# Six of the eight gate units of a retention mixer as three pairs by seven products, with the token sums kept in the retention results' memory

## The chip, the cores and the metric

The kernel runs on one core of a Trainium2 chip. It is one step of a small hybrid decoder: 512 prompt tokens and 8 sample tokens go through two layers. The metric is the device time of one execution in microseconds (us).

## The reference, cut to what matters

The change lies in the first layer's mixer, where the gate `g` is one of six parts of a combined input projection:

```python
h = rmsnorm(x, norm_mix_g[l])
z = h @ w_in                                   # (520 tokens, 1024) @ (1024, 5120)
q, k, v, g, u, s = jnp.split(z, SPLIT_IDX, axis=-1)   # widths 512, 512, 1024, 1024, 1024, 1024
...
o_n = ((o - mu) * lax.rsqrt(var + LN_EPS)).reshape(b, t, V_W) * gn_g
ret_out = jax.nn.silu(g) * o_n
```

All numbers are float32. The norm's factor is a number per token, so the kernel multiplies the weights by unnormalised rows and applies the factor `r0` to the products.

## The kernel before

**Layout.** Channels lie on the 128 partitions, tokens along the row: `x0` is [128, 8 chunks of channels, 520 tokens]. The 520 tokens are split into two halves of 260 columns (`HALF`), since a TensorE product writes one bank.

**A unit** is 128 output channels. Its weights arrive as one 512 KB transfer into `raw` (four buffers). `split` makes them into a high and a low part for half of the input channels at a time: ScalarE rounds (`wh`, L134), VectorE subtracts (`wl`, L135), each 128x512. The inputs are split in the same way into `n0h` and `n0l`. TensorE multiplies high by high, high by low and low by high: 8 chunks x 3 products x 2 halves = 48 matmuls of 260 columns, all in `unit_mm` (L163).

**A pair by seven products** is what the feed-forward stage uses already (`Pair`, `run`, L251). Two units whose weights form a 2x2 block matrix, by output unit and half of the input channels, meet tokens that form another, by half of the channels and half of the tokens. Seven products of sums in place of eight: 7 x 4 chunks x 3 = 84 matmuls instead of 96. It needs four sums of weights (`S`, VectorE, L236 to L239, 128x512 each), seven splits instead of four, the sums of tokens (`Tokens`, `T` high and low), and sums of the results, which are read from the banks `pp`, `pq`, `pr`. Products 2, 3 and 1 go on unsummed tokens; 5, 7, 6 and 4 on `Th`, `Tl`. Product 4 is left pending and done in the next pair, or by `flush`.

**Token sums** (`Tokens.sums(k)`, four calls): ScalarE scales one row (`Tu`, L206), VectorE makes four sums of 260 (`t4`, L209 to L212), and for two halves of the result ScalarE rounds (`Th`, L216) and VectorE subtracts (`Tl`, L217), 128x520 each.

**The stage around the change.** After the norm, units follow in this order: four for `k`, four for `q`, eight for the gate `g`, eight for `v`. For each `q` unit ScalarE makes two copies of 64 rows (`sw`), GpSimd multiplies `sw` by sines (L478) and later the result by `xi` (L489), and VectorE does the rest (L477, L479, `qm` L494, `qk_s` L618). For each gate unit VectorE multiplies the bank by `r0` (L502), ScalarE takes Silu (L503, with a load of its table before the first), and GpSimd multiplies by the norm's gain (L504) into `sg`.

**Order.** A scheduler at build time sets each engine's order and the semaphores; each engine then runs its list strictly in that order. **Memory.** The tag `big` has five buffers: `x0`, `n0h`, `n0l`, `sg`, `reth`, and `retl` takes the place of `x0`, whose last reader was the norm.

Of the kernel before, what the change touches and what calls it, by code (L numbers as in the profile page):

```python
# [6 lines left out]
F32 = mybir.dt.float32  # L7
F32R = mybir.dt.float32r
I32 = mybir.dt.int32
AF = mybir.ActivationFunctionType  # L10
ALU = mybir.AluOpType
# [3 lines left out]
P = 128  # L15
D = 1024
C = 8
TP = 512
TS = 8
T = TP + TS  # L20
HALF = T // 2
# [57 lines left out]
def trunk_kernel(tc, a, o):  # L79
    nc = tc.nc  # L80
    te, ve, se, pe_ = nc.tensor, nc.vector, nc.scalar, nc.gpsimd
    with ExitStack() as st:
# [10 lines left out]
        def open_stage(name):  # L93
            stage.close()
            return stage.enter_context(tc.tile_pool(name=name, bufs=2, reuse_waits="tile"))

        mp = open_stage("mix0")

        def bigt(name, dt=F32):
            return big.tile([P, C, T], dt, name=name, tag="big")  # L100
# [4 lines left out]
        def mmt(name):  # L105
            return ps.tile([P, 2, 512], F32, name=name, tag="mm", bufs=2)
# [10 lines left out]
        def h2(ap):  # L117
            return ap.rearrange("p (h t) -> p h t", h=2)

        def ph2(pt):  # L120
            return pt[:, :, :HALF]
# [7 lines left out]
        KH = C // 2  # L129
# [14 lines left out]
        def halves(pt):  # L144
            return [pt[:, hf, :HALF] for hf in range(2)]
# [9 lines left out]
        def unit_mm(pts, w, x, mid=None, ks=range(C), all_ks=None):  # L155

            order = list(all_ks or ks)
            for n, k in enumerate(ks):
                hi, lo = w[k // KH]
                for i in range(3):  # L160
                    wt = lo if i == 2 else hi
                    for hf in range(2):
                        last = te.matmul(pts[hf], wt[:, k % KH, :], x(k, SECOND if hf else FIRST)[i == 1],  # L163
                                         start=k == order[0] and i == 0, stop=k == order[-1] and i == 2)
                if mid and n == 4:
                    mid()
            return last

        def unit(pt, ap, row, col, x, mid=None, ks=range(C)):

            return unit_mm(halves(pt), split_w(load_w(ap, row, col)), x, mid=mid, ks=ks)
# [15 lines left out]

        T_OF = {5: 0, 7: 1, 6: 2, 4: 3}

        def four(name):  # L190
            return mp.tile([P, 4, HALF], F32, name=name, tag="f4", bufs=2)

        class Tokens:


            def __init__(self, x, nm):
                self.x, self.nm = x, nm
                self.b = two(nm.hi, nm.lo)
                self.t = [mp.tile([P, C, T], F32R, name="T" + s, tag="T", bufs=2)
                          .rearrange("p (k a) (b t) -> p k (a b) t", k=KH, b=2) for s in "hl"]  # L200

            def sums(self, k):
                t4 = four("t4")
                x, g1, g2 = self.x, pcol(self.nm.g, k), pcol(self.nm.g, KH + k)
                u = tmp("Tu")
                se.activation(u, x[:, k, :], AF.Copy, scale=g1)  # L206
                b21, b22 = x[:, KH + k, FIRST], x[:, KH + k, SECOND]
                stt = ve.scalar_tensor_tensor
                ve.tensor_sub(t4[:, 0], u[:, FIRST], u[:, SECOND])  # L209
                stt(out=t4[:, 1], in0=b22, scalar=g2, in1=u[:, SECOND], op0=ALU.mult, op1=ALU.subtract)  # L210
                stt(out=t4[:, 2], in0=b22, scalar=g2, in1=t4[:, 0], op0=ALU.mult, op1=ALU.add)
                stt(out=t4[:, 3], in0=b21, scalar=g2, in1=t4[:, 2], op0=ALU.mult, op1=ALU.subtract)  # L212
                hi, lo = [t[:, k] for t in self.t]
                for i, sign in enumerate((1.0, -1.0)):
                    s = slice(2 * i, 2 * i + 2)
                    se.activation(hi[:, s], t4[:, s], AF.Copy, scale=sign)  # L216
                    stt(out=lo[:, s], in0=t4[:, s], scalar=sign, in1=hi[:, s].bitcast(F32), op0=ALU.mult, op1=ALU.subtract)  # L217
# [39 lines left out]
        def flush():  # L257
            while pending:
                pending.pop().product(4)

        def run(pair, mid=None):
            if not pair.w:
                pair.load()
            pair.open()
            pair.product(1)
            flush()
            for n in (2, 3, 5, 6, 7) if pair.early else (2, 5, 6, 3, 7):
                if mid and n == (5 if pair.early else 3):
                    mid()
                pair.product(n)  # L270
            pending.append(pair)
# [11 lines left out]
        x0 = bigt("x0")  # L283
# [3 lines left out]
        def pcol(i, c):  # L287
            return par[:, i, c:c + 1]
# [121 lines left out]
        W_IN = a["ab_w_in"]  # L410
# [7 lines left out]
        nm = Norm(G_MIX0, "n0")  # L418
# [5 lines left out]
        xs0 = two(nm.hi, nm.lo)  # L424
# [12 lines left out]
        r0 = nm.r  # L437
# [13 lines left out]
        def in_units(first, n):  # L451
            for j in range(n):
                if first == 512 and j < 3:
                    pt = (k0, pt1, pt2)[j]
                else:
                    pt = mmt(f"in{first}_{j}")
                    unit(pt, W_IN, 0, first + j * P, xs0)
                yield j, pt
# [4 lines left out]
        def rot(pt, name, flat=False):  # L463
            sw = tmp(name + "sw")
            y = mp.tile([P, 544], F32, name=name, tag="qk", bufs=8)[:, :T]
            if isinstance(pt, list):
                parts = [(pt[hf], slice(hf * HALF, (hf + 1) * HALF)) for hf in range(2)]
            elif flat:
                parts = [(pt, slice(0, T))]
            else:  # L470
                parts = [(ph2(pt), None)]
            for src, cols in parts:
                def v(ap):
                    return h2(ap) if cols is None else ap[:, cols]
                se.copy(v(sw)[0:64], src[64:128])
                se.copy(v(sw)[64:128], src[0:64])
                ve.tensor_tensor(v(y), src, v(cs[:, 0, :]), op=ALU.mult)  # L477
            pe_.tensor_mul(sw, sw, cs[:, 1, :])  # L478
            ve.tensor_add(y, y, sw)  # L479
            return y  # L480

        kt, qt = [], []
        for h, pt in in_units(512, NH):
            y = rot(pt, f"k{h}", flat=h == 0)
            ve.tensor_scalar(ks[:, h, :], y[:, TP:], KSCALE, None, op0=ALU.mult)
            kt.append(y)
        for h, pt in in_units(0, NH):
            y = rot(pt, f"q{h}")
            pe_.tensor_tensor(y[:, :TP].rearrange("p (n t) -> p n t", n=NC), y[:, :TP].rearrange("p (n t) -> p n t", n=NC),  # L489
                              xi[:, h:h + 1, :].to_broadcast([P, NC, P]), op=ALU.mult)  # L490
            qt.append(y)
# [4 lines left out]


        sg = bigt("sg")
        reth, retl = bigt("reth", F32R), bigt("retl", F32R)
        for c, pt in in_units(2048, C):  # L500
            t = tmp(f"g{c}")
            ve.tensor_tensor(h2(t), ph2(pt), h2(r0), op=ALU.mult)  # L502
            se.activation(sg[:, c, :], t, AF.Silu)  # L503
            pe_.tensor_scalar(sg[:, c, :], sg[:, c, :], pcol(GN_G, c), None, op0=ALU.mult)  # L504


        def tok(n):
# [78 lines left out]
        for c, pt in in_units(1024, C):  # L586
            vT = tmp(f"vT{c}")
            ve.tensor_tensor(h2(vT), ph2(pt), h2(r0), op=ALU.mult)
            pe_.tensor_copy(vs_sm[:, c, :], vT[:, TP:])
            if prev:  # L590
                v_tok(*prev)
            prev = c, vT
            h = c // 2
            if c % 2 == 0:
                if h:
                    on[h - 1] = ret_head(h - 1, *pk[h - 1])
                if h > 1:
                    ret_gate(h - 2, on[h - 2])
                pk[h] = ret_scores(h)
# [99 lines left out]
        for hf in range(2):  # L699
            for i in range(2):  # L700
                t = mp.tile([P, 544], F32, name="ln_row", tag="qk", bufs=8)[:TS, :512]
# [37 lines left out]
        for c, pt in in_units(4096, C):  # L739
            t = tmp(f"s{c}")  # L740
# [18 lines left out]
        x = bigt("x")  # L759
# [13 lines left out]
        for c in range(2, C):  # L773
            pt = mmt(f"opr{c}")
# [14 lines left out]
        for c, pt in in_units(3072, C):  # L789
            g = c // 2  # L790
            t = tmp(f"u{c}")
            bias_c = mp.tile([P, TP], F32, name="bias_c", tag="on", bufs=4)[:, :P]
            ve.scalar_tensor_tensor(out=bias_c, in0=ws[:, g, :], scalar=pcol(SLN_B, c), in1=bias_row[:, g, :],
                                    op0=ALU.mult, op1=ALU.add)
# [3 lines left out]
            for n in range(NC):  # L798
# [6 lines left out]
                                    op0=ALU.mult, op1=ALU.add)  # L805
# [9 lines left out]
        for i in range(2):  # L815
            ht = mp.tile([P, nk, C, TS], F32, name="hist", tag="vtm", bufs=NH)
            nc.sync.dma_start(ht, a["hist"][:, i * nk:(i + 1) * nk])
            for c in range(C):
                pe_.tensor_tensor(ht[:, :, c, :], ht[:, :, c, :],
                                  dw[:, c, i * nk:(i + 1) * nk].rearrange("p (k o) -> p k o", o=1).to_broadcast([P, nk, TS]),  # L820
                                  op=ALU.mult)
# [6 lines left out]
        mp = open_stage("ffn0")  # L828


        nm = Norm(G_FFN0, "n1", eng=ve)
        x7 = Tokens(x, nm)
        ahead = Pair(a["ffn_w1"][0], 0, [u * KH * P for u in range(2)], x7, None, True)
        for c in BY_PAIR:
            if c == 2:
                ahead.load()
            pt = mmt(f"ops{c}")
# [135 lines left out]
        mp = open_stage("mix1")  # L973
# [4 lines left out]
        for c in range(CFULL, C):  # L978
            tag, bufs, parts = (("kx", 2, 2), ("s0", 3, 1), ("s0", 3, 1), ("s0", 3, 1), ("S", 1, 1))[c - CFULL]
            for i in range(parts):  # L980
                n = NS // parts
# [159 lines left out]
        mp = open_stage("ffn1")  # L1141
# [37 lines left out]
        nm = Norm(G_FFN1, "n3", eng=ve)  # L1179
        x7 = Tokens(x, nm)  # L1180
# [72 lines left out]
```

## Time and profile before

| | |
|---|---|
| runs, us | 1302.75, 1303.93, 1305.08 (median 1303.93) |
| the profiled execution | 1304.76 us, its span 1303.0 us |
| busy, share of the span | TensorE 98%, VectorE 68%, ScalarE 49%, GpSimd 14% |
| TensorE's mean granted clock | 0.993 |

The profile is of one execution. A row of a timeline gives start, duration, engine, line, operation, tiles and shapes, and in brackets how long the engine had been idle and for whom. A duration contains a part that overlaps the next instruction of the same engine, so what an engine can do in a stretch is read from the distance of two starts. In rows of groups, the number after the bar is busy time, then the mean duration in ns.

### The profile page before, as it was taken

What the parts mean: (1) busy time and instruction counts of PE and PEld (TensorE: products, weight loads), DVE (VectorE), ACT (ScalarE), POOL (GpSimd) and SP (SyncE); (2) the same over time, 40 slices, a digit from 0 to 9 for tenths busy, and PEclk for the clock granted to TensorE, in tenths of its full rate; (3) what the DMA queues carried; (4) which work ended last, traced back from release to release, by engine and by line L of the source; (5) the groups of instructions that cost most, each with busy time, mean ns of one, the idle gap of its engine ahead of it and who ended that gap; (6) DMA issues with size and microseconds to landing.
All of it is one profiled execution on the core that took longest, in us unless ns stands there. A gap on an engine that the chain in (4) does not pass through costs nothing.

```text
span 1303.0 us, 26234 instructions
## 1 busy us (share of the span) xinstructions
PE 1271.8 (98%) x10736; PEld 1237.5 (95%) x10736; DVE 891.2 (68%) x1628; ACT 638.7 (49%) x1148; POOL 183.1 (14%) x188
## 2 busy tenths in 40 slices
PE   9999999999999999999999999999899999999996
PEld 8999998999999999999999999868799999999996
DVE  6833667747888866766655799737987667576544
ACT  7433343335466644544434466347765445454342
POOL 0521012213000000000000479412000000000010
PEclk9999999999999999999999999999899999999998
DMA  8233235576423333333333324545333323332321
GB/s 284 88 92 97 76 111 182 177 233 224 137 81 99 98 98 98 98 100 96 98 98 98 93 87 118 147 99 149 110 98 98 114 82 108 104 98 81 98 81 66
DMA packets 51176, 149.62 MB, mean 115 GB/s; under 512 B 6081, under 2 KB 14401, under 8 KB 51057
## 3 DMA queue, kind: packets, MB, share of 16 engines
q1 hardware_dynamic: 46528, 134.37, 33.9%
q0 software_dynamic: 3456, 12.58, 2.9%
q8 instruction: 84, 1.38, 0.4%
q10 hardware_dynamic: 1072, 1.00, 0.2%
q14 instruction: 36, 0.29, 0.1%
HBM read 139.47 MB, written 9.41 MB: 114 GB/s over the span
## 4 chain that ended last, share of the span: by engine, by line
PE 86%; DVE 6%; POOL 4%; issue 2%; ACT 2%; DMA 0%; SPq 0%; DVEq 0%; ACTq 0%; POOLq 0%
PE y L163 27%; PE in L163 16%; PE pp L251 13%; PE pq L251 6%; POOL pacc L1052 3%; PE pr L251 3%; PE ops L163 3%; PE opr L163 3%; PE ci L163 2%; PE co L181 2%; PE f L163 2%; DVE wl L135 1%; PE cvB L1029 1%; PE cvA L1029 1%; PE opr L181 1%
## 5 line engine op out<-in xcount | busy, mean ns | idle before, releaser
L134 ACT ACTIVATE wh<-raw 128x512 fp32r<-128x512 f32 x378 | 237.0, 630 | 341.2 <-PE in L163 102.9
L135 DVE TENSOR_TENSOR wl<-raw,wh 128x512 fp32r<-128x512 f32 x378 | 274.5, 729 | 162.7 <-ACT wh L134 159.7
L163 PE MATMUL y<-f,wh 128*128 128x260 f32 x2016 | 324.0, 283 | 0.8 <-DVE x L912 0.8
L163 PEld LDWEIGHTS y<-f,wh 128*128 128x128 f32 x2016 | 275.7, 188 | 1.2 <-DVE x L912 1.2
L163 PE MATMUL y<-f,wl 128*128 128x260 f32 x1008 | 202.6, 282 | 0.0
L163 PEld LDWEIGHTS y<-f,wl 128*128 128x128 f32 x1008 | 155.3, 188 | 0.0
L163 PE MATMUL in<-n0h,wh 128*128 128x260 f32 x640 | 133.3, 288 | 1.4 <-DVE k L477 0.8
L163 PE MATMUL in<-n0l,wh 128*128 128x260 f32 x640 | 130.8, 285 | 1.0 <-DVE n0l L366 0.9
L163 PE MATMUL in<-n0h,wl 128*128 128x260 f32 x640 | 129.6, 284 | 0.1
L134 ACT ACTIVATE wh<-S 128x512 fp32r<-128x512 f32 x120 | 75.7, 632 | 96.6 <-PE y L163 45.6
L135 DVE TENSOR_TENSOR wl<-S,wh 128x512 fp32r<-128x512 f32 x120 | 82.2, 688 | 50.7 <-ACT wh L134 49.6
L163 PEld LDWEIGHTS in<-n0h,wh 128*128 128x128 f32 x640 | 99.0, 189 | 4.0 <-issue 1.9
L251 PE MATMUL pp<-Th,wh 128*128 128x260 f32 x360 | 101.9, 283 | 0.0
L251 PE MATMUL pp<-Tl,wh 128*128 128x260 f32 x360 | 101.4, 282 | 0.0
L251 PE MATMUL pp<-Th,wl 128*128 128x260 f32 x360 | 101.1, 282 | 0.0
L163 PEld LDWEIGHTS in<-n0l,wh 128*128 128x128 f32 x640 | 98.8, 188 | 2.4 <-DVE n0l L366 2.1
L163 PEld LDWEIGHTS in<-n0h,wl 128*128 128x128 f32 x640 | 98.5, 188 | 0.4 <-DVE wl L135 0.3
L251 PEld LDWEIGHTS pp<-Th,wh 128*128 128x128 f32 x360 | 67.9, 189 | 0.3 <-ACT wh L134 0.2
L251 PEld LDWEIGHTS pp<-Tl,wh 128*128 128x128 f32 x360 | 67.8, 188 | 0.1
L251 PEld LDWEIGHTS pp<-Th,wl 128*128 128x128 f32 x360 | 67.4, 188 | 0.0
L865 ACT ACTIVATE f<-f 128x520 fp32r<-128x520 f32 x60 | 38.4, 640 | 50.2 <-DVE f L864 50.2
L1052 POOL TENSOR_TENSOR pacc<-pacc,pp 128x512 f32<-128x512 f32 x39 | 59.5, 1530 | 4.0 <-ACT pp L1051 1.7
(410 smaller groups left out, 2771.9 us busy)
## 6 DMA issues: line engine op xcount, KB each, us to landing
raw<-in_ffn_w SPq DMA_DIRECT2D x128, 512.0 KB, 3.7
raw<-in_ab_w_in SPq DMA_DIRECT2D x39, 512.0 KB, 3.7
S<-in_state_ret POOLq DMA_DIRECT2D x16, 512.0 KB, 4.6
raw<-in_ab_w_out SPq DMA_DIRECT2D x16, 512.0 KB, 3.7
raw<-in_conv_w_in SPq DMA_DIRECT2D x16, 512.0 KB, 3.7
raw<-in_conv_w_out SPq DMA_DIRECT2D x16, 512.0 KB, 3.9
X<-xscr SPq DMA_DIRECT2D x40, 132.0 KB, 3.5
x<-in_xT SPq DMA_DIRECT2D x16, 260.0 KB, 4.5
```

The lines of the kernel that those rows point to most:

```text
L134: se.activation(hi, sp, AF.Copy)
L135: ve.tensor_sub(lo, sp, hi.bitcast(F32))
L163: last = te.matmul(pts[hf], wt[:, k % KH, :], x(k, SECOND if hf else FIRST)[i == 1], start=k == order[0] and i == 0, stop=k == order[-1] a ...
L181: te.matmul(pt, wt[:, k % KH, :], xt, start=n == 0 and i == 0, stop=n == C - 1 and i == 2)
L251: te.matmul(bank, wt[:, k, :], xt, start=(n in (1, 2, 5) or n == 3 and self.early) and k == 0 and i == 0, stop=k == KH - 1 and i == 2, ski ...
L865: se.activation(dst[:, 0, u], src, AF.Square)
L1029: te.matmul(acc[32 * g:32 * g + 32, :], diag[c, k][:, g, :], X[:, g, k:k + HC], start=k == 0, stop=k == ns - 1)
L1052: pe_.tensor_add(pacc, pacc, pp)
```

## The change

Gate units 0 and 4 stay as they are and go first. Units 1 and 5, 2 and 6, 3 and 7 become three pairs. The token sums of the first norm are made while the last two `q` units and gate units 0 and 4 are worked on; their high and low parts (`Th`, `Tl`) stand in the two `big` buffers that `reth` and `retl` had, so these two are allocated only after the last pair's pending product, in the first `v` unit. The 128x4x260 work tiles (`t4`, `f4`) share the three buffers of the tag `s0` with the retention's states.

```diff
-        def four(name):
-            return mp.tile([P, 4, HALF], F32, name=name, tag="f4", bufs=2)
+        def four(name, mixer=False):
+            return mp.tile([P, 4, HALF], F32, name=name, tag="s0" if mixer else "f4", bufs=3 if mixer else 2)
...
-                self.t = [mp.tile([P, C, T], F32R, name="T" + s, tag="T", bufs=2)
+                self.t = [(bigt("T" + s, F32R) if mixer else mp.tile([P, C, T], F32R, name="T" + s, tag="T", bufs=2))
...
+        x7 = Tokens(x0, nm, True)
         for h, pt in in_units(0, NH):
             y = rot(pt, f"q{h}")
+            if h >= 2:
+                x7.sums(h - 2)
...
         sg = bigt("sg")
-        reth, retl = bigt("reth", F32R), bigt("retl", F32R)
-        for c, pt in in_units(2048, C):
+
+        def g_row(c, t, sign):
+            se.activation(sg[:, c, :], t, AF.Silu, scale=sign)
+            pe_.tensor_scalar(sg[:, c, :], sg[:, c, :], pcol(GN_G, c), None, op0=ALU.mult)
+
+        def g_pair(i):
+            f4 = four("f4", True)
+            rows = f4.rearrange("p (u h) t -> p u (h t)", u=2)
+
+            def read(n, bank):
+                q = {1: 0, 2: 0, 6: 1, 3: 1, 4: 2, 5: 3, 7: 3}[n]
+                if n in (1, 6, 5, 4):
+                    se.copy(f4[:, q], bank)
+                else:
+                    ve.tensor_tensor(f4[:, q], bank, f4[:, q], op=ALU.add)
+                if n in (3, 4):
+                    u = n // 4
+                    ve.tensor_tensor(rows[:, u], rows[:, u], r0, op=ALU.mult)
+                    g_row(i + u * KH, rows[:, u], 1.0 - 2.0 * u)
+
+            run(Pair(W_IN, 0, [2048 + (i + u * KH) * P for u in range(2)], x7, read))
+
+        for c in (0, KH):
+            pt = mmt(f"in2048_{c}")
+            unit(pt, W_IN, 0, 2048 + c * P, xs0)
             t = tmp(f"g{c}")
             ve.tensor_tensor(h2(t), ph2(pt), h2(r0), op=ALU.mult)
-            se.activation(sg[:, c, :], t, AF.Silu)
-            pe_.tensor_scalar(sg[:, c, :], sg[:, c, :], pcol(GN_G, c), None, op0=ALU.mult)
+            g_row(c, t, 1.0)
+            x7.sums(2 + c // KH)
+        for i in range(1, KH):
+            g_pair(i)
...
+            if c == 0:
+                flush()
+                reth, retl = bigt("reth", F32R), bigt("retl", F32R)
```

The change moves instructions on all engines, since the scheduler orders them anew. With the two sum tiles allocated, the five `big` buffers are taken when `sg` comes; `sg` now stands in the place of `x0`, and its first row can be written only when the last token sum has read `x0`.

VectorE before, from the last `q` unit to the second gate unit (`q_718` is that unit's result, `g_792` and `g_855` are gate rows):

```order
L477 TENSOR_TENSOR q_718<-in_3_658,cs 128x520
L479 TENSOR_TENSOR q_718<-q_718,q3sw 128x520
L135 TENSOR_TENSOR wl<-raw,wh 128x512
L494 SCALAR_TENSOR_TENSOR qm<-q_718,qmask 128x64
L618 TENSOR_TENSOR qk_s<-q_718,ks 128x8
L502 TENSOR_TENSOR g_792<-in_0_733,n0r 128x520
L135 TENSOR_TENSOR wl<-raw,wh 128x512 x2
L502 TENSOR_TENSOR g_855<-in_1_796,n0r 128x520
```

VectorE now, from the second gate unit (gate unit 4, `g_888`) on (`t_892` is the work tile of the last token sum, `S_910` and `S_911` are weight sums of the first pair, `S_1032` of the second, `f_903` the first pair's result; the `wl` out of `raw` is of the second pair's first product):

```order
L528 TENSOR_TENSOR g_888<-in_4_829,n0r 128x520
L135 TENSOR_TENSOR wl<-S_911,wh 128x512
L209 TENSOR_TENSOR t_892<-Tu 128x260
L210 SCALAR_TENSOR_TENSOR t_892<-x_75,par,Tu 128x260
L217 SCALAR_TENSOR_TENSOR Tl<-t_818,Th 128x520
L135 TENSOR_TENSOR wl<-S_910,wh 128x512
L238 TENSOR_TENSOR S_1032<-S_1030,raw 128x512
L516 TENSOR_TENSOR f_903<-pr,f_903 128x260
L211 SCALAR_TENSOR_TENSOR t_892<-x_75,par,t_892 128x260
L135 TENSOR_TENSOR wl<-raw,wh 128x512
L217 SCALAR_TENSOR_TENSOR Tl<-t_892,Th 128x520
```

Where a gate unit had three rows on VectorE, token sums, weight sums and sums of results now stand between the splits of the weights.

ScalarE before, from the last `q` unit's splits to the second gate row:

```order
L134 ACTIVATE wh<-raw 128x512 x2
L503 ACT_TABLE_LOAD
L503 ACTIVATE sg<-g_792 128x520
L134 ACTIVATE wh<-raw 128x512 x2
L503 ACTIVATE sg<-g_855 128x520
```

ScalarE now, in the first pair:

```order
L216 ACTIVATE Th<-t_892 128x520
L134 ACTIVATE wh<-raw 128x512
L514 COPY f_1024<-pp 128x260
L134 ACTIVATE wh<-raw 128x512
L514 COPY f_903<-pq 128x260
L504 ACT_TABLE_LOAD
L504 ACTIVATE sg<-g_814 128x520
L504 ACTIVATE sg<-g_888 128x520
L216 ACTIVATE Th<-t_892 128x520
L134 ACTIVATE wh<-S_1029 128x512
```

The load of the table and the first two gate rows (`g_814`, `g_888`) moved from the gate units into the first pair, and stand between the two halves of the last token sum.

TensorE before, at the start of a gate unit:

```order
L163 MATMUL in_0_733<-n0h,wh 128x260 x2
L163 MATMUL in_0_733<-n0l,wh 128x260 x2
L163 MATMUL in_0_733<-n0h,wl 128x260 x2
L163 MATMUL in_0_733<-n0h,wh 128x260 x2
L163 MATMUL in_0_733<-n0l,wh 128x260 x2
```

TensorE now, in the first pair (banks `pp_916` and `pq_917`; `pp_1037` and `pq_1038` are the second pair's; `wh_953` is of product 5, `wh_987` of product 3, `wh_970` of product 6, `wl_1041` of the second pair's product 1):

```order
L251 MATMUL pq_917<-Th_457,wh_953 128x260
L251 MATMUL pp_1037<-n0h_112,wl_1041 128x260
...
L251 MATMUL pq_917<-Tl_458,wh_953 128x260
L251 MATMUL pq_917<-Th_457,wl_954 128x260
L251 MATMUL pq_917<-n0h_112,wh_987 128x260
...
L251 MATMUL pp_916<-Th_457,wh_970 128x260
L251 MATMUL pq_1038<-Th_457,wh_1094 128x260
```

The last quarters of products 5 and 6 are moved back behind the second pair's product 1 and the first pair's product 3, and product 3 follows product 5 in the same bank.

More of the change, by code (lines that the diff above doesn't have):

```diff
@@ L188, in trunk_kernel, with __init__ @@
         T_OF = {5: 0, 7: 1, 6: 2, 4: 3}
-        def four(name):
-            return mp.tile([P, 4, HALF], F32, name=name, tag="f4", bufs=2)
+        def four(name, mixer=False):
+            return mp.tile([P, 4, HALF], F32, name=name, tag="s0" if mixer else "f4", bufs=3 if mixer else 2)
         class Tokens:
-            def __init__(self, x, nm):
-                self.x, self.nm = x, nm
+            def __init__(self, x, nm, mixer=False):
+                self.x, self.nm, self.mixer = x, nm, mixer
                 self.b = two(nm.hi, nm.lo)
-                self.t = [mp.tile([P, C, T], F32R, name="T" + s, tag="T", bufs=2)
+                self.t = [(bigt("T" + s, F32R) if mixer else mp.tile([P, C, T], F32R, name="T" + s, tag="T", bufs=2))
                           .rearrange("p (k a) (b t) -> p k (a b) t", k=KH, b=2) for s in "hl"]
             def sums(self, k):
-                t4 = four("t4")
+                t4 = four("t4", self.mixer)
                 x, g1, g2 = self.x, pcol(self.nm.g, k), pcol(self.nm.g, KH + k)
```

## The prediction

> **What bounds the kernel now.** I read the page's busy shares first, then two windows over the stage, then the chain and the timelines of its engines. TensorE is the bound nearly everywhere. The first window below holds two `q` units and a part of the third, the second the last of it, the fourth, the eight gate units and most of the first `v` unit.
>
> ```profile
> PE 1271.8 (98%) x10736; PEld 1237.5 (95%) x10736; DVE 891.2 (68%) x1628; ACT 638.7 (49%) x1148; POOL 183.1 (14%) x188
> 41.05:59.00 17.95, 17.95 (x149) 17.95 (x150) 15.34 (x26) 6.71 (x11) 9.69 (x6) 1.00 0.32 97
> 59.00:110.50 51.50, 51.50 (x431) 51.50 (x430) 19.93 (x30) 18.51 (x30) 15.69 (x10) 1.00 0.32 92
> 41.05 69.42 PE in L163 x576
> 111.59 5.75 PE in L163 x48
> ```
>
> A window's columns are busy PE, PEld, DVE, ACT, POOL, then clock and DMA. TensorE never rests from 41.05 us on. A unit of 48 matmuls takes 5.75 us, so one matmul 0.12 us (the chain's 69.42 us are twelve units, 5.78 us with what lies between). VectorE (DVE) is at 85% in the `q` units and at 39% in the gate units: the change adds its work on VectorE just where the two meet.
>
> **What is saved.** Three pairs of 84 matmuls stand for six units of 48: 3 x 12 = 36 matmuls fewer, 36 x 0.12 = 4.3 us, all of it on TensorE's path. This is a third of a per cent; about 0.2% (2.6 us) either way is what a measurement of this kernel tells from no change.
>
> **What is added on VectorE, and its pace.** Nine splits more (25 for 16), 12 sums of weights, 9 sums of results, 16 sums of tokens and 8 `Tl`; the multiplications by `r0` stay eight. The pace is read from the distance of starts:
>
> ```profile
> 427.21 0.42 DVE L895 TENSOR_TENSOR f<-pr,f 128x260 f32<-128x260 f32 x1
> 427.55 0.68 DVE L135 TENSOR_TENSOR wl<-raw,wh 128x512 fp32r<-128x512 f32 x1
> 428.15 0.68 DVE L239 TENSOR_TENSOR S<-raw 128x512 f32<-128x512 f32 x1
> 422.03:441.22 19.19, 19.19 (x162) 19.19 (x162) 16.20 (x27) 14.48 (x29) 0.00 (x0) 1.00 0.22 65
> ```
>
> 260 columns take 0.34 us, 512 or 520 take 0.60. So 29 long and 25 short ones: 17.4 + 8.5 = 26 us, in a stage where VectorE has some 31 us free. A pair by itself is covered: 7 splits, 4 sums, 2 multiplications and 3 sums are 8.8 us against 84 x 0.12 = 10.1 on TensorE, and in the feed-forward stage, where a pair has two more long ones, the last window shows TensorE busy throughout. What is not evenly spread is the token sums, due before the first pair's products 5, 6, 7 and 4.
>
> **GpSimd in the `q` units holds VectorE up.**
>
> ```profile
> 45.27 0.68 DVE L477 TENSOR_TENSOR q<-in,cs 128x520 f32<-128x520 f32 x1
> 46.84 1.68 POOL L489 TENSOR_TENSOR q<-q,xi 128x512 f32<-128x512 f32 x1 [3.47 <-DVE q L479]
> 47.28 1.32 DVE L494 SCALAR_TENSOR_TENSOR qm<-q,qmask 128x64 f32<-128x64 f32 x1
> 48.52 0.15 DVE L618 TENSOR_TENSOR qk_s<-q,ks 128x8 f32<-128x8 f32 x1
> 32.79 1.65 POOL L478 TENSOR_TENSOR k0sw<-k0sw,cs 128x520 f32<-128x520 f32 x1
> 33.19 1.35 DVE L477 TENSOR_TENSOR k<-in,cs 128x520 f32<-128x520 f32 x3
> 60.36 1.30 POOL L478 TENSOR_TENSOR q3sw<-q3sw,cs 128x520 f32<-128x520 f32 x1 [1.97 <-ACT q3sw L476]
> 66.83 1.59 POOL L504 TENSOR_SCALAR sg<-sg,par 128x520 f32<-128x520 f32 x1 [2.67 <-ACT sg L503]
> 67.75 0.69 DVE L135 TENSOR_TENSOR wl<-raw,wh 128x512 fp32r<-128x512 f32 x1 [2.07 <-ACT wh L134]
> ```
>
> `qm`, 64 columns, needs some 0.15 us and took until GpSimd's two-operand instruction ended at 48.52: about 1.2 us blocked. Three instructions that read a bank (33.19) went at full pace beside one. Undisturbed, GpSimd's takes 1.30. The new weight sums, token sums and `Tl` all read two operands outside the banks, so they are blocked as `qm` is. The Trainium skill, "SBUF — State Buffer", section on practical consequences, says the same: a VectorE instruction with two SBUF inputs and a GpSimd instruction that reads SBUF exclude each other, one with a bank as input not. It would count the gate's gain (L504) among those that block; the row at 67.75, 0.69 us inside L504's 66.83 to 68.42, shows no block. I go by the row, and the rule's result is a rival below.
>
> **How late VectorE gets.** Up to the `q` unit's multiplication at 45.27 us VectorE's list is as before. From there I add up the new list to the split `wl_1041`, which TensorE needs for the second pair's first product (placed inside the first pair). TensorE would get there at: rest of that unit, 41.05 + 5.78 = 46.8; two `q` and two gate units, 4 x 5.78 = 23.1; 45 matmuls, 5.4; sum 75.3 us. VectorE has 12 splits, 7 weight sums, 8 rotary instructions, 6 `Tl` and 2 multiplications by `r0` = 35 x 0.605 = 21.2; 15 token sums and one of results at 0.34 = 5.4; four `qm`, `qk_s` at 0.22 = 0.9: 27.5 us. 45.3 + 27.5 = 72.8 without blocking: just in time. In this stretch GpSimd has seven two-operand instructions (four L489, three L478). VectorE is now never idle, so each costs it up to 1.30 us. Bounds: 0 if each fell beside an instruction that reads a bank (before 72.8: TensorE waits for nothing), 7 x 1.3 = 9.1 and 0.5 for a wait on ScalarE's copies (VectorE done at 82.4: TensorE 7.1 late). I take 1.2 each as at `qm`, 8.4 us, and the 0.5: 81.7, so TensorE loses 6.4 us, spread over the starts of `q3`, gate 0, gate 4 and the first pair. Near the upper end, as most of the list is of the blocked kind.
>
> **ScalarE's order in the first pair.**
>
> ```profile
> 64.79 1.28 ACT L503 ACT_TABLE_LOAD   x1
> 66.08 0.64 ACT L503 ACTIVATE sg<-g 128x520 f32<-128x520 f32 x1
> 67.08 0.63 ACT L134 ACTIVATE wh<-raw 128x512 fp32r<-128x512 f32 x1 [0.35 <-PE in L163]
> 428.24 0.36 ACT L893 COPY f<-pq 128x260 f32<-128x260 f32 x1
> 428.50 0.64 ACT L865 ACTIVATE f<-f 128x520 fp32r<-128x520 f32 x1
> 429.15 0.63 ACT L134 ACTIVATE wh<-raw 128x512 fp32r<-128x512 f32 x1
> 429.69 0.36 ACT L893 COPY f<-pp 128x260 f32<-128x260 f32 x1
> ```
>
> A split takes 0.54 from start to start, a copy 0.26. Two waits of TensorE lie in series here. (a) Product 3 goes into the bank of product 5, so it waits for the copy `f_903<-pq`. Ahead of that stand two splits and one copy. If TensorE comes late, the first of these splits waits for the very same matmuls (its buffer): 0.54 + 0.26 + 0.54 + 0.26 = 1.6, with the semaphores 1.7; if not, only the last copy, 0.4. I take 1.7, since TensorE is late by the step above. (b) After the copy come the table load, two gate rows and the second half of `Th`, for which product 6's last quarter waits: 1.28 + 3 x 0.6 = 3.1 us, while TensorE has product 3's 12 matmuls, 1.44: 1.6 us lost. Before, the load lay in ScalarE's free time in a gate unit. (c) The next split, `wh_1094`, stands behind that `Th` on ScalarE, and its `wl` behind it on VectorE: 0.54 + 0.60 less the matmuls between, about 0.8. At nothing: 0 for (c), and 0 for (b) if the load were early; nothing in the list allows that.
>
> The other added work of ScalarE (9 splits, 12 copies, 4 `Tu`, 8 `Th`: 4.9 + 3.1 + 2.4 + 4.8 = 15 us) is covered: it is busy 18.51 of 51.5 us. DMAs: none added, none reordered; a pair holds two of the four `raw` buffers until product 4, at 92 GB/s in the window above a light load. GpSimd's eight gains move later, to where `v` does not yet need them (`sg` is first read in the fifth `v` unit). From the second pair on nothing is late; behind the stage everything is shifted.
>
> **Sum:** -4.3 + 6.4 + 1.7 + 1.6 + 0.8 = +6.2 us. Against the profiled execution's 1304.76 that is 1311.0; the median of the runs, 1303.93, stands 0.8 below it, which gives 1310.1.
>
> **Rivals.** (1) VectorE in time: its blocks fall beside bank readers or beside waits, as before, where the `q` units' blocks cost TensorE nothing (its 17.95 of 17.95). Then (a) shrinks to 0.4, (c) may go; -4.3 + 0.4 + 1.6 + 0 to 0.8, about -2 us, 1302: no measurable change. It decides if no more than two of seven blocks cost VectorE; against it stands a list with no pause. (2) All hidden, faster: only the 36 matmuls count, 1299.6. It needs (b) hidden too, against the written order: TensorE would have to be over 1.6 us behind for a reason of its own. (3) Worse: L504 blocks VectorE too. Two gains per pair, 3.2 us, against a pair's 10.1 - 8.8 = 1.3 us of room: 1.9 us more per pair in one to three pairs, 1312 to 1316. The row at 67.75 speaks against it. (It is the result of the Trainium skill's rule above.) (4) The clock: a rest of TensorE brought half speed before:
>
> ```profile
> 826.85 0.48 PE L163 MATMUL ci<-n2h,wh 128*128 128x260 f32 x2 [3.10 <-DVE ca L1000]
> 828.00:832.00 4.00, 4.00 (x23) 0.57 1.04 186
> 400.19 0.39 PE L251 MATMUL pr<-n1h,wh 128*128 128x260 f32 x1 [1.24 <-DVE f L897]
> ```
>
> After 3.10 us of rest the clock was 0.57 over the next 4 us, 1.7 us lost; after 1.24 us nothing came. The rests here, by the steps above, are of some 2 us at most, so I expect none; with one, 1312. The Trainium skill, "TensorE: Matmul & The Clock Gate", Part 1, names an idle window of about 3.4 us; the 3.10 here is near that.
>
> **How the numbers follow.** My sum with its bounds, 1306.5 to 1313: 0.70. Worse, (3) or (4): 0.15. VectorE in time: 0.10. All hidden: 0.05. So slower 0.85, same 0.09, faster 0.06. The predicted time is 1310.1; the range 1305.0 to 1314.0 leaves out the hidden cases and the worst of (3).
>
> **What the new profile would show.** Right: 10700 matmuls for 10736, the `in` groups at 544 for 640, L251 up by 252; TensorE idle some 10 us between 50 and 95 us, with DVE `wl` or `Tl` as releaser for the larger part and ACT `Th` and `wh` for the rest; DVE over 95% busy from 50 to 85; L212, L217 or the weight sums with means well over 0.69 us. Wrong: TensorE at 99% there (rivals 1 and 2), or waits in the second and third pair (rival 3), or a clock below 1.00 before 120 us (rival 4). I would be wrong most easily in the size of the blocking, which hangs on where GpSimd's instructions fall.

## The result, and the profile after

The changed kernel takes 1312.28 us (median; 1310.65 to 1313.4), the kernel before 1303.52 in the same series: 1.0063 times, 95% interval 1.0050 to 1.0075, so 8.8 us slower. Forecast were 6.2 us more. The profiled execution took 1313.4 us, its span 1311.7 against 1303.0.

The first line of the page after, and the two windows of the prediction again (busy PE, PEld, DVE, ACT, POOL, then clock and DMA):

```profile
PE 1272.0 (97%) x10700; PEld 1236.2 (94%) x10700; DVE 918.4 (70%) x1682; ACT 653.6 (50%) x1181; POOL 185.0 (14%) x188
41.05:59.00 17.95, 17.30 (x144) 17.10 (x143) 15.89 (x26) 6.27 (x11) 8.35 (x5) 1.00 0.30 89
59.00:110.50 51.50, 44.71 (x347) 42.98 (x347) 44.55 (x78) 30.36 (x56) 15.98 (x10) 0.97 0.26 77
```

The 36 matmuls are gone. In these 69.45 us TensorE started 491 matmuls where it had started 580, and was idle for 7.44 us where it had never been. 89 x 0.12 = 10.7 us lost, less the 4.3 saved: 6.4 us. The clock's column, 0.97, holds a half-speed stretch of 3.4 us that the prediction did not expect.

Where the rest came shows in two landmarks that both programs have behind the stage, the last copy of `v_s` and the matmul of the dots. First before, then after (start, duration, engine, line):

```profile
179.38 0.57 ACT L606 COPY v_s<-vst 8x512 f32<-8x512 f32 x1
187.62 1.70 ACT L653 ACTIVATE vb<-vb,ks 128x256 f32<-128x256 f32 x4 [2.98 <-DMA vb<-scr]
190.14 0.34 PE L622 MATMUL dots<-one_col,qk_s 128*8 128x1 f32 x8
```

```profile
185.64 0.57 ACT L637 COPY v_s<-vst 8x512 f32<-8x512 f32 x1
195.54 1.71 ACT L684 ACTIVATE vb<-vb,ks 128x256 f32<-128x256 f32 x4 [4.61 <-DMA vb<-scr]
197.77 0.35 PE L653 MATMUL dots<-one_col,qk_s 128*8 128x1 f32 x8 [1.28 <-ACT on L579]
```

At `v_s` the program stands 6.26 us later, at the dots 7.63, at its end 8.7. The start was shorter, though: VectorE's last `k` row, up to which its list is as before, came 0.59 us earlier (before, then after):

```profile
40.22 0.69 DVE L477 TENSOR_TENSOR k<-in,cs 128x520 f32<-128x520 f32 x1
39.63 0.69 DVE L477 TENSOR_TENSOR k<-in,cs 128x520 f32<-128x520 f32 x1
```

So the stage cost 6.26 + 0.59 = 6.85 us, a little more than the 6.2 forecast, and 2.4 us came behind it: 1.4 because ScalarE stood 4.61 us for the transfer `vb` (2.98 before), 1.0 further on.

TensorE's waits in the stage (line waited for: us in total, times, longest):

```profile
PE in L163 <- DVE q L477: 1.6, 2, 0.9
PE pq L251 <- ACT f L514: 1.4, 1, 1.4
PE pp L251 <- ACT f L514: 1.3, 1, 1.3
PE pp L251 <- ACT Th L216: 1.3, 1, 1.3
PE pp L251 <- DVE wl L135: 1.3, 1, 1.3
PE pq L251 <- DVE Tl L217: 0.3, 1, 0.3
```

They fall between 58 and 88 us; in the second and third pair there is none. VectorE's list in the same stretch, the rows that stand out and the split `wl_1041` at its end:

```profile
44.67 0.68 DVE L477 TENSOR_TENSOR q<-in,cs 128x520 f32<-128x520 f32 x1
46.68 1.32 DVE L497 SCALAR_TENSOR_TENSOR qm<-q,qmask 128x64 f32<-128x64 f32 x1
50.63 0.69 DVE L236 TENSOR_TENSOR S<-raw 128x512 f32<-128x512 f32 x1 [1.95 <-DMA raw<-in_ab_w_in]
53.66 1.78 DVE L238 TENSOR_TENSOR S<-S,raw 128x512 f32<-128x512 f32 x1
55.36 1.80 DVE L239 TENSOR_TENSOR S<-raw 128x512 f32<-128x512 f32 x1
60.86 1.51 DVE L212 SCALAR_TENSOR_TENSOR t<-x,par,t 128x260 f32<-128x260 f32 x1
65.56 0.94 DVE L209 TENSOR_TENSOR t<-Tu 128x260 f32<-128x260 f32 x1
69.58 1.28 DVE L649 TENSOR_TENSOR qk_s<-q,ks 128x8 f32<-128x8 f32 x1
81.06 0.68 DVE L135 TENSOR_TENSOR wl<-raw,wh 128x512 fp32r<-128x512 f32 x1
```

Six rows are longer than their size needs, by 1.1, 1.1, 1.1, 1.0, 0.5 and 1.1 us: 6.0 us of blocks. The first weight sum waits 1.95 us for the first pair's weights, with the whole list behind it. `wl_1041` is done at 81.7 us, and TensorE, which has stood 1.28 us for it, goes on with the second pair's first product at 81.80.

ScalarE's order in the first pair:

```profile
83.18 0.63 ACT L134 ACTIVATE wh<-raw 128x512 fp32r<-128x512 f32 x1 [3.91 <-PE pp L251]
83.72 0.36 ACT L514 COPY f<-pp 128x260 f32<-128x260 f32 x1
83.97 0.63 ACT L134 ACTIVATE wh<-raw 128x512 fp32r<-128x512 f32 x1
84.50 0.36 ACT L514 COPY f<-pq 128x260 f32<-128x260 f32 x1
84.89 1.28 ACT L504 ACT_TABLE_LOAD   x1
86.18 1.16 ACT L504 ACTIVATE sg<-g 128x520 f32<-128x520 f32 x2
87.25 0.62 ACT L216 ACTIVATE Th<-t 128x520 fp32r<-128x520 f32 x1
```

Product 3 waited for the copy at 84.50 (1.42 us), product 6's last quarter for the `Th` at 87.25 (1.31 us). The wait of 1.34 us for a copy in the other bank came earlier, at 77.55: that copy stood on ScalarE behind a `Th` which had waited 1.45 us for VectorE's token sum.

### The profile page after: what moved, and what is told of

Same layout as the page of the kernel before. It is cut to its first block, busy times and chain, and to the rows that moved or that the text cites. A ratio compares the mean times of both kernels' runs of the same rounds, so it can differ in the third digit from the quotient of the medians.

```text
span 1311.7 us, 26247 instructions
## 1 busy us (share of the span) xinstructions
PE 1272.0 (97%) x10700; PEld 1236.2 (94%) x10700; DVE 918.4 (70%) x1682; ACT 653.6 (50%) x1181; POOL 185.0 (14%) x188
## 4 chain that ended last, share of the span: by engine, by line
PE 81%; DVE 7%; POOL 4%; ACT 3%; issue 3%; DMA 2%; DVEq 0%; SPq 0%; ACTq 0%
PE y L163 27%; PE pp L251 14%; PE in L163 11%; PE pq L251 7%; PE pr L251 4%; POOL pacc L1083 3%; PE ops L163 3%; PE opr L163 3%; PE ci L163 2%; PE f L163 2%; DVE wl L135 2%; PE co L181 1%; PE cvB L1060 1%; PE cvA L1060 1%; PE opr L181 1%
## 5 line engine op out<-in xcount | busy, mean ns | idle before, releaser
L135 DVE TENSOR_TENSOR wl<-S,wh 128x512 fp32r<-128x512 f32 x132 | 90.5, 688 | 49.9 <-ACT wh L134 49.0
L163 PE MATMUL in<-n0h,wh 128*128 128x260 f32 x544 | 114.3, 289 | 3.0 <-DVE q L477 1.6
L251 PE MATMUL pp<-Th,wh 128*128 128x260 f32 x396 | 113.0, 286 | 2.7 <-ACT f L514 1.3
L163 PE MATMUL in<-n0l,wh 128*128 128x260 f32 x544 | 111.8, 286 | 0.8 <-DVE n0l L366 0.6
L251 PE MATMUL pp<-Tl,wh 128*128 128x260 f32 x396 | 112.3, 284 | 0.0
L251 PE MATMUL pp<-Th,wl 128*128 128x260 f32 x396 | 112.0, 284 | 0.0
L163 PE MATMUL in<-n0h,wl 128*128 128x260 f32 x544 | 110.2, 284 | 0.1
L163 PEld LDWEIGHTS in<-n0h,wh 128*128 128x128 f32 x544 | 84.1, 189 | 5.8 <-PE in L163 3.5
L163 PEld LDWEIGHTS in<-n0l,wh 128*128 128x128 f32 x544 | 84.1, 188 | 2.2 <-DVE n0l L366 1.9
L163 PEld LDWEIGHTS in<-n0h,wl 128*128 128x128 f32 x544 | 83.7, 188 | 0.4 <-DVE wl L135 0.3
```

The source lines that it names most:

```text
L135: ve.tensor_sub(lo, sp, hi.bitcast(F32))
L251: te.matmul(bank, wt[:, k, :], xt, start=(n in (1, 2, 5) or n == 3 and self.early) and k == 0 and i == 0, stop=k == KH - 1 and i == 2, ski ...
```

## The experiments

Theory 1 is the prediction's: token sums and GpSimd's blocks make VectorE late, and ScalarE's order in the first pair adds to it. Against it stood that the pairs themselves cost the time (theory 2), and that the clock and waits behind the stage do (theory 3). Each time is a median; each ratio is to the kernel before in the same series, with its 95% interval. "At `v_s`" gives the time of that landmark, which is at 179.38 us before. The start differs from profile to profile (the last `k` row is between 39.31 and 40.26 us); "less the start" takes the shift of that row, against 40.22 us, off the shift of the landmark. With the changed kernel the landmark is 6.85 us later, less the start.

**Pairs without token sums**

```diff
-                if n in T_OF:
+                if n in T_OF and not self.mixer:
...
-            if h >= 2:
-                x7.sums(h - 2)
```

(and the other two calls; all products then read the unsummed rows)

> Left out: the token sums (16 sums, 8 Tl, 4 Tu, 8 Th); all seven products of a pair read rows of the first norm, so the result is not the reference's. What is left of the change is the three pairs with their weight sums, their seven products and their bank waits. Theory 1 (the loss is made in VectorE's list by the token sums, 16 x 0.4 + 8 x 0.6 = 11 us of work and the GpSimd blocks that fall on it): most of the 6.3 us go; the 36 matmuls less are left with at most 1 us for blocked weight sums and up to 1.6 us for ScalarE's order: 1300 to 1303 us, equal to the kernel before or up to 3.5 us faster. Theory 2 (the pairs themselves cost it: weight sums, bank of product 3, table load): 1308 to 1312 us. Theory 3 (the half-speed stretch at 77.7 us and what is lost behind the stage): TensorE is still late before 80 us by the weight sums, and the time stays above 1306.

1300.6 us, 0.9972 (0.9962 to 0.9982); at `v_s` 175.44, 3.94 us earlier than before, 3.4 less the start. The three pairs alone bring most of what 36 matmuls are worth, 4.3 us. From 45 us on TensorE has one wait, 0.6 us for VectorE's `q`, and none in the pairs. Theories 2 and 3 fall for the stage. ScalarE's order is not tested here: without `Th` it is another one, with the table's load (65.12 us) and the first gate rows ahead of the pairs.

**GpSimd's two-operand work in the `q` units left out**

```diff
-            pe_.tensor_mul(sw, sw, cs[:, 1, :])
+            if name[0] == "k":
+                pe_.tensor_mul(sw, sw, cs[:, 1, :])
...
-            pe_.tensor_tensor(y[:, :TP]..., y[:, :TP]..., xi[:, h:h + 1, :]..., op=ALU.mult)
```

> Left out: GpSimd's two-operand work in the four q units (the product with the second half of the angles and the decay xi), so the result is not the reference's; VectorE, ScalarE and TensorE have the same lists as in the changed kernel. Theory 1 (VectorE's list from 45 to 82 us is full, and GpSimd's two-operand instructions stop it for some 6 us): VectorE is done with the second weight split of the second pair 5 to 6 us earlier, and the time is 1306 us (1305 to 1308). Rival (the blocks fall beside waits that VectorE would have anyway, and its own work and the wait for the first pair's weights set the time): 1311 to 1312.5.

1304.67 us, 1.0004 (0.9995 to 1.0013), a little below the range expected; at `v_s` 179.38, just where it was before, 0.75 us later less the start. The blocks were worth 6.1 us of TensorE's time. Its waits from 59 us on, with those for `q` and `Tl` and the one at 77.55 gone:

```profile
PE pq L251 <- ACT f L513: 1.4, 1, 1.4
PE pp L251 <- ACT Th L216: 1.3, 1, 1.3
PE pp L251 <- DVE wl L135: 0.7, 1, 0.7
```

The same work left out of the kernel before is the control:

> Control: the same work of GpSimd left out of the kernel before the change; the result is not the reference's. VectorE waited for GpSimd there too, but TensorE never did (17.95 of 17.95 us busy), so all theories of the q units expect no change: 1302.7 to 1305 us. If it comes out faster by over 1.3 us, the gain of the changed kernel without this work was not the end of the blocks of its sums.

1304.34 us, 1.0001 (0.9991 to 1.0010), at `v_s` 179.00, unchanged (0.02 us) less the start. The blocks cost nothing while VectorE has slack.

**GpSimd's work with one operand in place of two**

```diff
-            pe_.tensor_mul(sw, sw, cs[:, 1, :])
+            if name[0] == "k":
+                pe_.tensor_mul(sw, sw, cs[:, 1, :])
+            else:
+                pe_.tensor_scalar(sw, sw, pcol(GN_G, 0), None, op0=ALU.mult)
...
-            pe_.tensor_tensor(y[:, :TP]..., y[:, :TP]..., xi[:, h:h + 1, :]..., op=ALU.mult)
+            pe_.tensor_scalar(y[:, :TP], y[:, :TP], pcol(GN_G, h), None, op0=ALU.mult)
```

> GpSimd's eight instructions with two operands in the q units become products with one column of parameters, on the same tiles, as those of the gate (L504) are; the result is not the reference's. VectorE still waits for GpSimd's results, and GpSimd is as busy as before or busier (1.6 us for 520 columns). Theory 1 (what stops VectorE is that both engines read two operands outside the banks): as without this work, 1304 to 1306.5 us, and VectorE's 512-column rows beside GpSimd's last 0.69. Rival 1 (VectorE waits for GpSimd's result, not for its port): 1310 to 1312. Rival 2 (every GpSimd instruction that reads SBUF stops VectorE's two-operand ones, as the Trainium skill, "SBUF — State Buffer", states): 1311 to 1313, with VectorE rows of over 1 us beside the new products.

1305.38 us, 1.0008 (0.9999 to 1.0018); at `v_s` 180.37. Less the start that is 0.95 us later than before the change, 0.2 behind the kernel without this work and 5.9 ahead of the changed one. Five rows of its timeline, two of GpSimd, three of VectorE:

```profile
59.62 2.69 POOL L495 TENSOR_SCALAR q<-q,par 128x512 f32<-128x512 f32 x1 [2.50 <-DVE q L482]
60.28 0.68 DVE L135 TENSOR_TENSOR wl<-raw,wh 128x512 fp32r<-128x512 f32 x1
61.85 0.48 DVE L210 SCALAR_TENSOR_TENSOR t<-x,par,Tu 128x260 f32<-128x260 f32 x1
62.29 1.83 POOL L481 TENSOR_SCALAR q3sw<-q3sw,par 128x520 f32<-128x520 f32 x1
62.67 1.10 DVE L135 TENSOR_TENSOR wl<-raw,wh 128x512 fp32r<-128x512 f32 x1
```

Two of VectorE's two-operand rows go at full pace inside GpSimd's first instruction, which itself takes 2.69 us, at its fastest 1.60 (46.60 us). The row at 62.67, inside the second, is held up by 0.4 us; rows at 42.76, 54.11 and 55.75 us are held up by 0.4, 0.4 and 0.3, and no row up to 82 us by more. So what stops VectorE until GpSimd is done is GpSimd's form with two operands, not the dependence on GpSimd's results; beside GpSimd's one-operand instructions VectorE loses some 1.2 us from its first `q` row on, against 6.0. The Trainium skill, "SBUF — State Buffer", practical consequences, lets any GpSimd instruction that reads SBUF contend with a VectorE instruction of two SBUF inputs. Here the two do disturb each other, but with GpSimd's one-operand form VectorE does not stand until GpSimd is done; the rows decide.

**The first pair's weight sums later in VectorE's list**

```diff
-                ve.tensor_add(s1, a21, a22)
+                with tc.issue_after(lo_ins[-1].ins) if self.x7.mixer else nullcontext():
+                    ve.tensor_add(s1, a21, a22)
```

(and the other three sums likewise; `lo_ins` are the subtractions of `split`)

> The changed kernel with one rule more: the first pair's four weight sums come behind the last weight split of gate unit 4 in VectorE's list, where in the changed kernel the first of them stands in the second q unit and waits 1.95 us there for the pair's weights (50.63 us). Nothing is left out. Theory 1 (VectorE's list is full from there to 82 us, so each us it stands still is lost): the 1.95 us and the two blocks of about 1.1 us on the sums come back, at most 3 us, less a wait before the first pair's product 5: 1309 to 1310.5 us. Rival (the list has to wait for GpSimd or ScalarE later on anyway): 1311.5 to 1312.5.

1308.65 us, 1.0038 (1.0026 to 1.0051), below the range expected; at `v_s` 183.28, 2.6 us earlier than in the changed kernel less the start. `wl_1041` is done at 78.8 us, 2.9 us earlier. The blocks did not go away: there are six again, of 6.0 us, one still on a weight sum (57.75 us). What changed is that three waits of 1.3 us together stand for the one of 1.95, and that two weight sums, a token sum and a `Tl` (2.2 us of work) moved behind `wl_1041`. So VectorE's list up to that split sets the time, as Theory 1 has it; that the wait for the weights alone is lost like a block is not shown, since the rest of the list moved with it. A half-speed stretch of 6.8 us from 79.6 us on took a part of the gain.

**ScalarE's order in the first pair: the table earlier**

```diff
+            if c == 0:
+                table(AF.Silu, t[:, :1])
             g_row(c, t, 1.0)
```

> One instruction more: ScalarE's table for the gate is loaded in gate unit 0, as before the change, not between the copy of product 6 and the second half of Th. Everything else as in the changed kernel. Theory 1 (ScalarE's order (b) is on TensorE's path): the 1.28 us of the load go out of the wait of 1.31 us at 87.92, and the time is 1311.0 us against 1312.3. Rival (TensorE waits there for VectorE anyway, or the time comes back as a wait in the next product): no difference, 1312 to 1313.

1309.7 us, 1.0042 (1.0029 to 1.0055); at `v_s` 184.87, 1.1 us earlier than in the changed kernel less the start. The wait for `Th` is gone, and 0.7 us of waits for the next `wh` and `wl` came in its place. The time is below both forecasts, as the loss at the dots is missing here too (see the changed kernel again, below).

**Product 3 in another bank, alone and with the early table**

```diff
-                bank = self.banks[2 if n == 2 or n == 3 and self.early else 1 if n in (5, 3) else 0]
+                bank = self.banks[2 if n == 2 or n == 3 and (self.early or self.x7.mixer) else 1 if n in (5, 3) else 0]
```

(and `start` of the matmul likewise)

> Product 3 of the gate's pairs goes into the bank of product 2 and starts it anew, so it waits for VectorE's sum of an earlier product and not for ScalarE's copy of product 5; the sum of the second row leaves product 5 out, so the result is not the reference's. The order of TensorE's list changes with it: product 3 comes ahead of the second pair's first product. Theory of the prediction (waits (a) and (b) of ScalarE's order lie in series): 1.4 us less, 1310.5 us. Rival (both hang on one chain of ScalarE, which ends with the second half of Th at 87.9 us; without (a) TensorE gets there earlier and waits longer): 1311.5 to 1312.5 us, with a wait of 2 us or more on Th.

> Both edits together: product 3 in the bank of product 2 (product 5 left out of the second row, so the result is not the reference's), and ScalarE's table loaded in gate unit 0. Theory of the prediction (in series): 1.4 us below the kernel with the early table alone, 1308.3 us. Rival (one chain): ScalarE's chain is shorter by the 1.28 us of the load and what (a) gives is again lost at Th: 1309.3 to 1310 us.

1311.29 us, 1.0064 (1.0050 to 1.0079), and 1309.88 us, 1.0046 (1.0033 to 1.0058): no gain by either that can be told from noise. At `v_s` 186.81 and 185.31; less the start that is 1.5 and 0.5 us later than without the edit. TensorE's wait for `Th` in the one and the other:

```profile
PE pp L251 <- ACT Th L216: 3.4, 1, 3.4
```

```profile
PE pp L251 <- ACT Th L216: 1.9, 1, 1.9
```

The wait grew from 1.31 to 3.36 us, and from nothing to 1.94 beside the early table: most of the 1.4 us is lost again at the next thing that ScalarE's one list delivers. The edit takes out more than (a), since TensorE's list changed with it: the wait for `wl_1041` is gone too, and product 3 waits 0.91 us for VectorE's sum. Measured from the wait for `Tl` shortly before it, `Th` is reached 0.6 us earlier in both. That rest was then taken by a half-speed stretch of the clock right behind it, 3.4 us long in the second kernel, 6.8 in the first, whose windows these are:

```profile
82.76:86.17 3.41, 0.54 (x5) 0.33 (x3) 1.25 (x2) 3.17 (x5) 0.52 (x1) 1.00 0.49 161
86.17:93.00 6.83, 6.19 (x27) 5.90 (x28) 5.54 (x9) 3.02 (x7) 2.64 (x2) 0.50 0.23 76
```

So the times came out about as the rival said (the first 0.2 us below its range), by two causes of which it had named one.

**The changed kernel again**

> The changed kernel once more, nothing edited. In its first profile 6.3 us were lost up to the end of the pairs, and 2.3 us behind them: 1.4 us at the matmul of the dots, where ScalarE stood behind a transfer (vb) that landed 1.6 us later than before, and the rest in the convolution, where the half-speed stretch of the clock lasted 10.2 us for 6.8. Theory 1 (what is lost behind the stage belongs to that execution): this profile shows 6.3 us at the end of the pairs and less than 1 us behind, and the time is 1310 to 1311 us. Rival (the shift of the program brings the transfer and the clock's stretch with it): again 1.3 us at the dots, 1312 to 1313.

1311.78 us, 1.0054 (1.0035 to 1.0072). At `v_s` 186.60, 7.2 us later than before, 7.8 less the start; at the dots 1.2 us more again, with ScalarE standing 4.46 us for `vb`. Theory 1 was wrong here: the loss at the dots belongs to this program. It was also there without token sums (4.62 us), with the weight sums later (4.44) and with the other bank and the early table together (4.11), and not with the early table (3.27), with the other bank alone (2.60), with GpSimd's one-operand work (3.21), without that work (2.89) or in the orders below (2.93 and 3.04). So whole times are compared with care here, and `v_s` tells what the stage did. What sets how long the little transfer ahead of `vb` takes was not tried and stays open.

**Another order: sums and pairs later**

```diff
+        def at(place):
+            for k in range(KH):
+                if (2, 3, 4, 5)[k] == place:
+                    with tc.issue_after(splits[-1].ins):
+                        x7.sums(k)
...
-            x7.sums(2 + c // KH)
-        for i in range(1, KH):
-            g_pair(i)
+            at(2 + c // KH)
...
+            at(4 + c)
...
+            if c == 1:
+                for i in range(1, KH):
+                    g_pair(i)
+                flush()
+                reth, retl = bigt("reth", F32R), bigt("retl", F32R)
```

(with the weight sums held as above, and `Tu` in the buffers of `v_tm`)

> The same work in another order: the token sums of the four groups stand in gate units 0 and 4 and v units 0 and 1, each held behind the last weight split on ScalarE, the three pairs come behind v unit 1, and the first pair's weight sums are held behind the last split on VectorE. Nothing is left out. Theory 1 (it was the token sums in the q units, where GpSimd blocks VectorE): VectorE has room, TensorE keeps the 36 matmuls less (4.3 us) but for one or two short waits in q3 and ScalarE's order in the first pair: 1300 to 1302.5 us, faster than before by 1 to 3.5 us. Theory 2 (the pairs themselves cost): their price is paid wherever they stand: 1308 or more. Theory 3 (clock, and waits behind the stage): 1304 to 1307.

1298.56 us, 0.9960 (0.9946 to 0.9974); at `v_s` 174.29, 5.1 us earlier than before the change, 4.35 less the start: just the 36 matmuls. The same two windows of this kernel:

```profile
41.05:59.00 17.95, 17.95 (x152) 17.95 (x152) 16.91 (x29) 8.44 (x14) 8.13 (x6) 1.00 0.28 89
59.00:110.50 51.50, 51.50 (x432) 51.41 (x431) 45.64 (x81) 30.32 (x57) 15.82 (x14) 1.00 0.31 98
```

VectorE is as busy as in the changed kernel (45.64 for 44.55 us), but TensorE never waits for it. ScalarE's order is another one too: the load and the last `Th` (79.93 us) are done ahead of the first pair's first copy.

```profile
77.56 1.28 ACT L516 ACT_TABLE_LOAD   x1 [3.31 <-DVE t L216]
84.51 0.36 ACT L526 COPY f<-pp 128x260 f32<-128x260 f32 x1
```

The edit moves several things at once, so it shows that the same work fits, not which of the moves was needed. The time is below the range expected, in part since the start, up to the first `k` units, was 0.7 us shorter than in the profile of before; in the control, which has nothing changed there, it was 0.4 us shorter.

**All eight gate units as four pairs, behind `v` unit 3**

```diff
-                if (2, 3, 4, 5)[k] == place:
+                if (4, 5, 6, 7)[k] == place:
...
-            if c == 1:
-                for i in range(1, KH):
+            if c == 3:
+                for i in (0, 1, 2, 3):
```

(and gate units 0 and 4 no longer by themselves)

> All eight gate units as four pairs behind v unit 3, the token sums one group each in v units 0 to 3, nothing left out. Against the kernel with three pairs behind v unit 1 (1298.6 us) it has 12 matmuls less, 1.4 us, and no sums near the q units. Theory 1 (only VectorE's list in the q units made the loss): 1296 to 1298 us. Rival (v units 2 and 3 have the retention's own work on VectorE and ScalarE, and the sums or the first pair come late there): 1299 to 1302 us.

1298.46 us, 0.9949 (0.9934 to 0.9963), half a microsecond above the range expected; at `v_s` 173.10, 5.9 us earlier than before less the start. TensorE has no wait in these units here either, and the 12 matmuls show in the landmark as 1.5 us; in the whole time the two orders can't be told apart. Both beat the kernel before and the changed one.

## Why the prediction was right, and where it was not

**The saving**, 36 x 0.12 = 4.3 us: right. With sums and pairs later, where TensorE has no wait, the landmark moved by 4.35 us less the start.

**"GpSimd in the `q` units holds VectorE up" and "How late VectorE gets"**, +6.4 us: right, and shown by taking the cause away: 6.1 us. `wl_1041` was forecast for 81.7 and ended at 81.7. Its terms were partly luck: 6.0 us of blocks for 8.4 (six, not seven: one of GpSimd's instructions fell into a pause of VectorE), a start 0.6 us earlier, and instead 1.95 us for the first pair's weights, which I had not seen since no weight sum stood in the old list, and three of four token sums at 0.40 from start to start where 0.34 was taken. By name, VectorE released 3.2 us of TensorE's waits in the stage and ScalarE 4.1, while the prediction looked for VectorE behind the larger part. The wait at 77.55 explains it: there VectorE's lateness came through a copy of ScalarE. VectorE was busy 95% of the time from 50 to 85 us, as forecast.

**"ScalarE's order"**, (a) 1.7, (b) 1.6, (c) 0.8: right in size. The waits of (a) and (b) were 1.42 and 1.31, with what a rest adds (0.26 each, see the last section) 1.7 and 1.6. (c) was two rests too short to be listed as waits, for the next `wh` and for its `wl`, together about 0.7 us:

```profile
88.45 0.39 PE L251 MATMUL pq<-Th,wh 128*128 128x260 f32 x1
89.27 0.39 PE L251 MATMUL pq<-Th,wl 128*128 128x260 f32 x1
```

With GpSimd's work left out all three were still there (1.42, 1.30 and the same two rests), though TensorE then stood only 0.74 us for `wl_1041`. So they are a price of this order as long as TensorE is late at all. What would be left of them with TensorE quite in time stays open: the runs without such waits have another order on ScalarE. What did not hold is to read "lie in series" as two prices of which each could be saved by itself: they are one list of ScalarE, and with (a) removed, most of it came back at (b). In the second profile of the changed kernel they were 1.13 us and nothing, while TensorE was at half speed.

**"After 1.24 us nothing came ... so I expect none"**, on the clock: failed. In the changed kernel half speed began at 77.6 us:

```profile
74.15:77.56 3.41, 1.76 (x14) 1.34 (x12) 3.41 (x7) 1.97 (x5) 0.00 (x0) 1.00 0.00 0
77.56:80.98 3.42, 2.95 (x12) 2.65 (x12) 3.42 (x8) 1.11 (x2) 0.00 (x0) 0.50 0.00 0
```

It cost little, since TensorE then waited for `wl_1041` anyway: in the kernel with the early table, with no half speed there, that wait was 1.92 us in place of 1.28. In the second profile the stretch began at 78.7 us and was 10.2 us long, and `v_s` came 1.0 us later than in the first.

**"Behind the stage everything is shifted"**: this is the 2.4 us by which the sum is short. 1.4 us are the transfer at the dots, in both profiles of this kernel. The last 1.0 us lie in the feed-forward and convolution stages, beside a half-speed stretch of 10.2 us (from 944.6 us) for 6.8 before; it was not traced further. The sum 6.2 and the 8.8 measured thus differ by 0.6 us in the stage, 2.4 behind it, and 0.6 less at the start, near enough.

Rival (1) gave the right mechanism for the experiment with GpSimd's work out, but 1302 for 1304.7: TensorE was still late for `wl_1041`, and (a) did not shrink to 0.4. Rival (3) is refuted by the experiment with one operand, where GpSimd held no row of VectorE up for more than 0.4 us, and by the second and third pair, where TensorE never waited.

## What to carry to other kernels

A count of matmuls saved is worth its time only while the helping engines' lists have slack at the place where the new work is due: the same pairs cost 8.8 us with their sums in the `q` units and gained 5 to 6 us in the two later orders. Before adding work to an engine, add up its list from the last point where it waited, with what another engine's two-operand work blocks and what its first operand's transfer takes. Waits of TensorE for one list of another engine may all be paid, and summing them gave the right size here; but what removing one of them gains is found from the list's end, not from that wait.

## What was not expected of the hardware

TensorE fell to half speed without a long rest: in the 3.41 us ahead of it, it had worked 1.76 us, with no wait over 1.34. The Trainium skill, "TensorE: Matmul & The Clock Gate", Part 1, names an idle window of some 3.4 us; here a half-idle one of that length was enough, though not always: in the same kernel it worked 1.71 us of the 3.41 from 80.98 us and 1.69 of the next 3.42, and kept full speed. Which it is stays open. The half-speed stretches in the stage, where a run had one, lasted 3.4, 6.8 or 10.2 us.

A rest of TensorE costs more than the wait in its row, by these profiles, in which the ends of matmuls are modelled. The matmul after one shows 0.39 us for 0.28, the next starts 0.22 us later for 0.12, and the row ahead of it reads 0.28 us where its slot is 0.12: some 0.26 us for each. Nine such rests (the seven waits, and two too short for one), 2.3 us, and 12 matmuls at half speed, 1.1 us, make 7.44 us of idle time the 10.7 us lost.
